# A hybrid decoder step: another order of the mixers, and convolution taps as ScalarE products with wide VectorE adds

## The chip, the cores and the metric

The kernel runs on one core of a Trainium2 chip. The metric is the time of one execution on the device in microseconds (us), lower being better; the time before is the median of three runs. A profile is one execution taken by the hardware profiler. The engines are TensorE (PE, with its weight loads PEld), VectorE (DVE), ScalarE (ACT), GpSimd (POOL) and SyncE (SP), which here only issues transfers. Each engine works through its own instructions in order and waits on semaphores for the others.

## What is computed

256 prompt rows and 8 sample rows, 264 in all, go through one layer of width D = 2048, everything in fp32:

```python
xn = rms_norm(x, g_mix)
z = xn @ w_in      # pool u 512 | lru x 1024 | gelu gate 1024 | conformer a 512 | conformer b 512
# A: trailing means over 2/4/8/16 rows minus the row, a 128x128 map per group, a scale, @ w_pool_br
# B: causal depthwise convolution, 4 taps -> gates -> recurrence h = a*h + b, times gelu, @ w_lru_br
gate_r, gate_i = sigmoid(xb @ w_a + b_a), sigmoid(xb @ w_x + b_x)
log_a = -8 * gate_r * softplus(-lam)
b = x * gate_i * sqrt(-expm1(2 * log_a))
# C: v = a * sigmoid(b) -> causal depthwise convolution, 31 taps -> LayerNorm -> swish -> @ w_conf_br
gates = sigmoid(xn @ w_gate + b_gate)
x = x + (g_a * y_pool + g_b * y_lru + g_c * y_conf) @ w_out
x = x + square(relu(rms_norm(x, g_mlp) @ w_up)) @ w_down
y = rms_norm(x, g_final)
```

The new rows of the states (pooling inputs, both convolutions' inputs, the recurrence's last h) are outputs too.

## The kernel before

Everything on the chip is transposed: channels on the 128 partitions, the 264 rows along the free axis, so a product is a 128x128 weight tile with a 128x264 moving tile, summed in one of eight PSUM banks.

**The weight stream.** All dense weights come as chunks of 128x1024 (two k tiles for four output tiles). `weight_plan` lists the groups of chunks in the order in which TensorE goes through them: 56 chunks of `w_in`, then gates, branch projections, `w_out`, `w_up`, `w_down`. fp32 precision comes from splitting: ScalarE casts a chunk to its high part `whi` (`split`, L148), VectorE subtracts that to get the low part `wlo` (L149), and `mm3` (L152 to L154) makes three products per tile: high x high, high x low, low x high. A chunk is 24 products. The split of chunk i+3 is issued at chunk i (`AHEAD`); the rings of high and low parts have four slots (`NHI`), that of raw weights six, and SP loads pairs of chunks by `dma_pair`.

**x at the start.** `x_tile` splits one k tile of x into `A` (L228 or L230, and L231) and forms its squares, on GpSimd for the first four tiles and on ScalarE after (L262), summed on GpSimd (L264, L266). After chunk 9 `rms_close` multiplies the total by a matrix of ones on TensorE, and ScalarE and VectorE make the inverse root `rstd` of it (a seed by Ln and Exp and a Newton step, L215 to L218). The first group of `w_in`, the conformer's b, is finished before `rstd` exists: its evacuation is a copy (L432), and GpSimd scales it afterwards (L436).

**Background work.** What the mixers do between products is put in four queues of stages (`stage`): each task has an engine and a planned cost. At every chunk `run_bg` adds an income to each engine's credit (1.3 us for ScalarE, 1.4 for VectorE, 2.4 for GpSimd) and issues tasks in order while the credit lasts; a stage begins at least one chunk after the one before it, unless its gap is 0. `later(n, fn)` issues something n chunks on. The finished evacuations and gates take their cost off by `spend`. None of this is decided at run time: it fixes the order in which each engine gets its instructions.

- `lru_conv`: three of four taps are scalar_tensor_tensor operations on VectorE, one per channel tile (L317).
- `conf`: of 30 taps (beside the first), 14 (`TAPS`) are such operations on VectorE (L455) and 16 are products on ScalarE (L460) with sums on GpSimd (L463).
- `lru_tail`: a and sqrt(1 - a*a) are made of tanh and a reciprocal on VectorE (L395), products of two tiles on GpSimd (L377), the scan on VectorE (L380). `gelu` multiplies on GpSimd (L413).
- `pooling`: four doubling adds on GpSimd (L559), differences on VectorE (L571 to L576); `grp_mm` is the group map.

The order of `w_in` before: conformer b, conformer a, lru x (two groups), pool, gelu (two groups). The gate matrices' blocks of the recurrence (`lru_gate_mm`) follow chunks of the gelu groups (`LRU_AT`). Gates and projections then alternate; `branch_evac` multiplies a projection by its gate, GpSimd adds the branches up (L621), and the sum is split for `w_out`.

**The end.** The last products are three with the matrix of ones (L833), which sum the squares of the result. ScalarE and VectorE make the inverse root, VectorE scales the result in seven pieces (L842), and SP sends each one out (L843).

Of the kernel before, what the change touches and what calls it, by code (L numbers as in the profile page):

```python
# [308 lines left out]

# [622 lines left out]
```

## Time and profile before

| | |
|---|---|
| median of 3 runs | 1448.97 us (1448.65 to 1449.99) |
| the profiled execution's span | 1448.0 us |
| TensorE busy | 1407.7 us, 11418 products |
| VectorE busy | 850.1 us, 1060 instructions |
| ScalarE busy | 684.4 us, 931 instructions |
| GpSimd busy | 230.8 us, 235 instructions |

How to read the profile's lines: "L149 DVE TENSOR_TENSOR wlo<-raw,whi 128x1024 ... x480" is a group of instructions of line 149 on VectorE that write the tile wlo from raw and whi; then come their busy time, the mean ns of one, and the idle time of that engine before them with what ended it. A row of three durations with slashes gives the shortest, median and longest ns. A line of digits shows the span in 40 equal slices, each digit the busy share in tenths; PEclk is the granted TensorE clock in tenths. A row of a stretch gives its start and end, its length, and the busy time and instruction count of each engine. A timeline row begins with the start and the time taken, in us. A row of a wait names the engine, tile and line that waited, what ended the wait, and the total, the count and the longest in us. Products are pipelined and their ends modelled, so a busy TensorE isn't always TensorE at its full rate.

### The profile page before, as it was taken

What the parts mean: (1) busy time and instruction counts of PE and PEld (TensorE: products, weight loads), DVE (VectorE), ACT (ScalarE), POOL (GpSimd) and SP (SyncE); (2) the same over time, 40 slices, a digit from 0 to 9 for tenths busy, and PEclk for the clock granted to TensorE, in tenths of its full rate; (3) what the DMA queues carried; (4) which work ended last, traced back from release to release, by engine and by line L of the source; (5) the groups of instructions that cost most, each with busy time, mean ns of one, the idle gap of its engine ahead of it and who ended that gap; (6) DMA issues with size and microseconds to landing.
All of it is one profiled execution on the core that took longest, in us unless ns stands there. A gap on an engine that the chain in (4) does not pass through costs nothing.

```text
span 1448.0 us, 26716 instructions
## 1 busy us (share of the span) xinstructions
PE 1407.7 (97%) x11418; PEld 1400.4 (97%) x11418; DVE 850.1 (59%) x1060; ACT 684.4 (47%) x931; POOL 230.8 (16%) x235
## 2 busy tenths in 40 slices
PE   8988889999999999999999999999999999999996
PEld 7987889999999999999999999999999999999996
DVE  8599978855654545565655445454455554454543
ACT  6665468455444434354544334453334533354543
POOL 5577641432220200211000000000000000000011
PEclk9999999999999999999999999999999999999998
DMA  7533445555565555555555555555555555555551
GB/s 274 196 126 136 141 145 188 204 175 175 179 218 186 175 175 180 188 186 176 175 178 182 189 180 175 178 181 187 184 175 175 179 188 187 175 176 178 185 189 62
DMA packets 38567, 256.96 MB, mean 177 GB/s; under 512 B 4272, under 2 KB 5040, under 8 KB 9008
## 3 DMA queue, kind: packets, MB, share of 16 engines
q1 hardware_dynamic: 38304, 254.21, 52.0%
q8 instruction: 89, 1.46, 0.4%
q0 software_dynamic: 144, 1.04, 0.2%
q14 instruction: 30, 0.25, 0.0%
HBM read 252.03 MB, written 3.21 MB: 176 GB/s over the span
## 4 chain that ended last, share of the span: by engine, by line
PE 89%; DVE 7%; issue 2%; ACT 1%; DMA 0%; SPq 0%; DVEq 0%; ACTq 0%
PE acc L154 30%; PE acc L152 30%; PE acc L153 30%; DVE wlo L149 3%; DVE G L455 2%; DVE G L317 1%; DMA GX<-x_dram 0%; ACT whi L148 0%; DVE GX L842 0%; DVE A L231 0%; DVE L L342 0%; ACT G L312 0%; ACT A L230 0%; ACT G L450 0%; SPq L135 0%
## 5 line engine op out<-in xcount | busy, mean ns | idle before, releaser
L149 DVE TENSOR_TENSOR wlo<-raw,whi 128x1024 fp32r<-128x1024 f32 (+1 forms) x480 | 600.5, 1252 | 569.5 <-ACT whi L148 566.4
L148 ACT CAST whi<-raw 128x1024 fp32r<-128x1024 f32 (+1 forms) x480 | 497.7, 1038 | 688.4 <-PE acc L153 667.3
L154 PE MATMUL acc<-A,wlo 128*128 128x264 f32 x2236 | 640.9, 287 | 16.3 <-DVE wlo L149 16.2
L152 PE MATMUL acc<-A,whi 128*128 128x264 f32 x2236 | 640.8, 287 | 6.5 <-DVE tmp L406 5.9
L153 PE MATMUL acc<-A,whi 128*128 128x264 f32 x2236 | 638.6, 286 | 3.4 <-DVE A L231 3.4
L154 PEld LDWEIGHTS acc<-A,wlo 128*128 128x128 f32 x2236 | 424.7, 190 | 19.8 <-DVE wlo L149 19.8
L152 PEld LDWEIGHTS acc<-A,whi 128*128 128x128 f32 x2236 | 424.5, 190 | 7.0 <-issue 6.8
L153 PEld LDWEIGHTS acc<-A,whi 128*128 128x128 f32 x2236 | 425.4, 190 | 5.2 <-DVE A L231 5.1
L152 PE MATMUL acc<-mrg,whi 128*128 128x264 f32 x768 | 218.8, 285 | 0.0
L154 PE MATMUL acc<-mrg,wlo 128*128 128x264 f32 x768 | 218.5, 284 | 0.0
L153 PE MATMUL acc<-mrg,whi 128*128 128x264 f32 x768 | 218.1, 284 | 0.0
L154 PE MATMUL acc<-L,wlo 128*128 128x264 f32 x656 | 187.0, 285 | 0.9 <-DVE wlo L149 0.9
L152 PE MATMUL acc<-L,whi 128*128 128x264 f32 x656 | 186.5, 284 | 0.0
L153 PE MATMUL acc<-Q,whi 128*128 128x264 f32 x644 | 182.7, 284 | 0.0
L667 POOL TENSOR_TENSOR G<-G 128x264 f32<-128x264 f32 x28 | 25.7, 917 | 811.8 <-ACT G L665 810.9
L153 PEld LDWEIGHTS acc<-mrg,whi 128*128 128x128 f32 x768 | 145.1, 189 | 0.0
L154 PEld LDWEIGHTS acc<-mrg,wlo 128*128 128x128 f32 x768 | 144.9, 189 | 0.0
L152 PEld LDWEIGHTS acc<-mrg,whi 128*128 128x128 f32 x768 | 144.7, 188 | 0.0
L154 PEld LDWEIGHTS acc<-L,wlo 128*128 128x128 f32 x656 | 123.5, 188 | 1.1 <-DVE wlo L149 1.1
L152 PEld LDWEIGHTS acc<-L,whi 128*128 128x128 f32 x656 | 123.4, 188 | 0.0
L153 PEld LDWEIGHTS acc<-Q,whi 128*128 128x128 f32 x644 | 121.5, 189 | 0.0
L621 POOL TENSOR_TENSOR G<-G 128x264 f32<-128x264 f32 x32 | 31.0, 999 | 228.4 <-DVE G L618 228.4
(154 smaller groups left out, 870.1 us busy)
## 6 DMA issues: line engine op xcount, KB each, us to landing
raw<-wall_dram SPq DMA_DIRECT2D x230, 1024.0 KB, 4.9
raw<-wall_dram SPq DMA_DIRECT2D x11, 512.0 KB, 7.6
GX<-x_dram SPq DMA_DIRECT2D x7, 264.0 KB, 7.8
raw<-wall_dram SPq DMA_DIRECT2D x7, 256.0 KB, 3.2
y_dram<-GX SPq DMA_DIRECT2D x2, 528.0 KB, 2.8
so_dram<-st POOLq DMA_DIRECT2D x1, 1018.0 KB, 6.9
st<-st_dram SPq DMA_DIRECT2D x1, 912.0 KB, 8.0
y_dram<-GX SPq DMA_DIRECT2D x3, 132.0 KB, 1.8
```

The lines of the kernel that those rows point to most:

```text
L148: nc.scalar.copy(h[:, s], r[:, s])
L149: nc.vector.tensor_tensor(lo[:, s], r[:, s], f(h[:, s]), op=ALU.subtract)
L152: nc.tensor.matmul(ps[:, :N], whi_t, xh, start=first, stop=False)
L153: nc.tensor.matmul(ps[:, :N], whi_t, xl, start=False, stop=False)
L154: nc.tensor.matmul(ps[:, :N], wlo_t, xh, start=False, stop=last)
L317: nc.vector.scalar_tensor_tensor(XC[:, ct, :TP], el[:, ct, k:k + TP], par[:, w:w + 1], XC[:, ct, :TP], op0=ALU.mult, op1=ALU.add)
L455: nc.vector.scalar_tensor_tensor(VC[:, ct, :TP], vext[:, ct, k:k + TP], par[:, w:w + 1], VC[:, ct, :TP], op0=ALU.mult, op1=ALU.add)
L621: nc.gpsimd.tensor_tensor(t, t, G[:, (1 - g % 2) * 12 + br * 4 - 4 + m, :], op=ALU.add)
L667: nc.gpsimd.tensor_tensor(sq2, sq2, t, op=ALU.add)
```

## The change

- The order of `w_in` becomes lru x (two groups), pool, gelu (two groups), conformer b, conformer a. The gates are regrouped: the conformer's come last, and the four conformer projections stand together before `w_out`. The recurrence's gate blocks all lie in the second gelu group.
- The taps of both convolutions become products on ScalarE, one per channel tile, into two alternating tiles; VectorE adds each set of four channel tiles with one wide instruction (`gather`).
- In the recurrence the reciprocals go: with u = tanh(-log(a) / 2) as before and a itself from an exponential on ScalarE, sqrt(1 - a*a) is (1 + a) sqrt(u), and a for the scan is 1 - (1 + a) u; the multiplications move from GpSimd to VectorE, as do those of `gelu` and of the conformer's b.
- Squares of x are no longer formed in `x_tile` but at chunks 5 to 8, four tiles at a time on ScalarE (`x_squares`), with VectorE adds; `x_rms` folds them after chunk 9. The first group's evacuation is now a copy of lru x, scaled afterwards by `lru_x_scale`.
- Queues are three with a fixed priority, planned costs are raised, and ScalarE's income is 1.6 until the recurrence is done, then 1.3 (VectorE's 1.4, then 1.0).
- Partial sums of the branches get tiles of their own (`partial`), the merged sum and the MLP's hidden halves go to other tiles (`A`, `LH`).
- After the last products with the matrix of ones, 32 products into a bank that nobody reads (`probe`) are issued.

The diff, cut to its core:

```diff
-LRU_AT = ((3, 5), (3, 7), (4, 1), (4, 3))  # chunks of w_in that the blocks of the LRU gates follow
-TAPS = 14      # conformer taps on the vector engine
...
+LRU_AT = ((4, 1), (4, 3), (4, 5), (4, 6))
...
-    groups = [("w_in", 0, 16, m) for m in (6, 5, 1, 2, 0, 3, 4)]
-    groups += [("w_gate", 0, 16, br * 4 + g) for g in (0, 1) for br in range(3)]
+    groups = [("w_in", 0, 16, m) for m in (1, 2, 0, 3, 4, 6, 5)]
     for g in range(4):
-        if g >= 2:
-            groups += [("w_gate", 0, 16, br * 4 + g) for br in range(3)]
-        groups += [("w_pool_br", 0, 4, g), ("w_lru_br", 0, 8, g), ("w_conf_br", 0, 4, g)]
+        groups += [("w_gate", 0, 16, t) for t in ((0, 4, 1), (5,), (2, 6), (3, 7))[g]]
+        groups += [("w_pool_br", 0, 4, g), ("w_lru_br", 0, 8, g)]
+    groups += [("w_gate", 0, 16, 8 + g) for g in range(4)]
+    groups += [("w_conf_br", 0, 4, g) for g in range(4)]
...
-    queues = {"pool": [], "lru": [], "conf": [], "conf2": []}
+    queues = {"lru": [], "pool": [], "conf": []}
     ready_at = dict.fromkeys(queues, 0)
     credit = {"act": 0.0, "dve": 0.0, "pool": 0.0}
-    income = {"act": 1.3, "dve": 1.4, "pool": 2.4}
+    income = {"act": 1.6, "dve": 1.4, "pool": 2.4}
...
+        if "lru" in done:
+            income.update(act=1.3, dve=1.0)
...
+    sq4 = G[:, 20:24, :]
     def x_tile(k):
         split_scaled(A[:, k, :], A[:, 16 + k, :], X[:, k, :], GX[:, k:k + 1], k < 2)
-        t = sq_tot if k == 0 else G[:, 21 + k % 3, :]
-        if k >= 4:
-            nc.scalar.activation(t, X[:, k, :], AF.Square)
-        else:
-            nc.gpsimd.tensor_tensor(t, X[:, k, :], X[:, k, :], op=ALU.mult)
-        if k:
-            nc.gpsimd.tensor_tensor(sq_tot, sq_tot, t, op=ALU.add)
-    # ---- softplus(-lambda) * LRU_C / 2
+    def x_squares(j):
...
+        t = sq4 if j == 0 else G[:, 4 * (j % 2):4 * (j % 2) + 4, :]
+        nc.scalar.activation(t, X[:, 4 * j:4 * j + 4, :], AF.Square)
+        spend(act=1.1)
+        def add():
+            nc.vector.tensor_tensor(sq4, sq4, t, op=ALU.add)
+            spend(dve=1.25)
+        if j:
+            later(1, add)
+    def x_rms():
+        nc.vector.tensor_tensor(sq4[:, 0:2, :], sq4[:, 0:2, :], sq4[:, 2:4, :], op=ALU.add)
+        nc.vector.tensor_tensor(sq4[:, 0, :], sq4[:, 0, :], sq4[:, 1, :], op=ALU.add)
+        spend(dve=1.2)
+        rms_close(sq4[:, 0, :])
+        later(1, lru_x_scale)
...
+    def lru_x_copy(ct, ps):
+        nc.vector.tensor_copy(el[:, ct, 3:], ps[:, :TP])
+        nc.vector.tensor_copy(st_lc[:, ct, :, 3], ps[:, TP:N])
+        spend(dve=0.5)
+    def lru_x_scale():
+        for d, r in ((el[:, 0:4, 3:], rstd[:, None, :TP]), (st_lc[:, 0:4, :, 3], rstd[:, None, TP:])):
+            nc.vector.tensor_tensor(d, d, r.to_broadcast([P, 4, d.shape[2]]), op=ALU.mult)
+        spend(dve=1.4)
+        lru_conv(range(4))
...
+        def product(ct, k, dst):
             w = w0 + 4 * ct + k
-            nc.vector.scalar_tensor_tensor(XC[:, ct, :TP], el[:, ct, k:k + TP], par[:, w:w + 1], XC[:, ct, :TP],
-                                           op0=ALU.mult, op1=ALU.add)
-        stage("lru", "act", 0.4, [lambda ct=ct: first(ct) for ct in cts])
-        stage("lru", "dve", 0.41, [lambda ct=ct, k=k: tap(ct, k) for k in range(3) for ct in cts], 0)
+            nc.scalar.activation(dst[:, ct, :TP], el[:, ct, k:k + TP], AF.Copy, scale=par[:, w:w + 1])
+        def gather(src):
+            nc.vector.tensor_tensor(XC[:, cs, :TP], XC[:, cs, :TP], src[:, cs, :TP], op=ALU.add)
+        stage("lru", "act", 0.5, [lambda ct=ct: first(ct) for ct in cts], 0)
+        for k in range(3):
+            dst = (RA, GEL)[k % 2]
+            stage("lru", "act", 0.5, [lambda ct=ct, k=k, d=dst: product(ct, k, d) for ct in cts], 0 if k == 0 else 1)
+            if k:
+                stage("lru", "dve", 1.25, [lambda d=(RA, GEL)[1 - k % 2]: gather(d)], 0)
+        stage("lru", "dve", 1.25, [lambda: gather(RA)])
...
+        if ct % 2:
+            def times():
+                nc.vector.tensor_tensor(XC[:, ct - 1:ct + 1, :], XC[:, ct - 1:ct + 1, :], TM[:, ct - 1:ct + 1, :],
+                                        op=ALU.mult)
+                spend(dve=0.71)
+            later(1, times)
...
+        def decay(ct):
+            nc.scalar.activation(RA[:, ct, :], RA[:, ct, :], AF.Exp, scale=sp[:, 8 + ct:9 + ct])
+        def reset():
+            nc.gpsimd.memset(TM[:, :, 0:1], 1.0)
+            nc.gpsimd.memset(RA[:, :, 0:1], 0.0)
         def root(c):
-            nc.scalar.activation(TM[:, two(c), :], TM[:, two(c), :], AF.Sqrt, scale=4.0)
+            if not S:
+                scratch()
+            nc.scalar.activation(S[0][:, two(c), :], TM[:, two(c), :], AF.Sqrt)
...
+        def wide(c, dst, x):
+            nc.vector.scalar_tensor_tensor(dst[:, two(c), :], RA[:, two(c), :], 1.0, x[:, two(c), :],
+                                           op0=ALU.add, op1=ALU.mult)
         def a_of(c):
-            nc.vector.tensor_scalar(RA[:, two(c), :], RA[:, two(c), :], 2.0, -1.0, op0=ALU.mult, op1=ALU.add)
-        def times(c, t):
-            nc.gpsimd.tensor_tensor(TM[:, two(c), :], TM[:, two(c), :], t[:, two(c), :], op=ALU.mult)
+            nc.vector.tensor_scalar(TM[:, two(c), :], TM[:, two(c), :], -1.0, 1.0, op0=ALU.mult, op1=ALU.add)
+        def times(c):
+            nc.vector.tensor_tensor(RA[:, two(c), :], RA[:, two(c), :], XC[:, two(c), :], op=ALU.mult)
...
-        stage("lru", "act", 0.4, [lambda ct=ct: tanh(ct) for ct in range(8)])
-        stage("lru", "pool", 0.1, [lambda: nc.gpsimd.memset(TM[:, :, 0:1], 1.0)])
-        stage("lru", "act", 0.55, [lambda c=c: nc.scalar.activation(RA[:, two(c), :], TM[:, two(c), :], AF.Copy, bias=1.0)
-                                   for c in range(4)], 0)
-        stage("lru", "act", 0.55, [lambda c=c: root(c) for c in range(4)], 0)
-        stage("lru", "dve", 0.9, [lambda s=s: nc.vector.reciprocal(s, s) for ct in range(8)
-                                  for s in (RA[:, ct, :N // 2], RA[:, ct, N // 2:])])
-        stage("lru", "pool", 1.26, [lambda c=c: times(c, RA) for c in range(4)])
-        stage("lru", "pool", 1.26, [lambda c=c: times(c, XC) for c in range(4)], 0)
+        c4 = range(4)
+        stage("lru", "act", 0.52, [lambda ct=ct: tanh(ct) for ct in range(8)], 0)
+        stage("lru", "act", 0.52, [lambda ct=ct: decay(ct) for ct in range(8)])
+        stage("lru", "pool", 0.2, [reset])
+        stage("lru", "act", 0.65, [lambda c=c: root(c) for c in c4])
+        stage("lru", "dve", 0.75, [lambda c=c: wide(c, TM, TM) for c in c4], 0)
+        stage("lru", "dve", 0.43, [lambda c=c: a_of(c) for c in c4], 0)
+        stage("lru", "dve", 0.75, [lambda c=c: wide(c, RA, S[0]) for c in c4], 0)
+        stage("lru", "dve", 0.71, [lambda c=c: times(c) for c in c4], 0)
         mark("lru", "b_term")
-        stage("lru", "dve", 0.35, [lambda c=c: a_of(c) for c in range(4)])
-        stage("lru", "dve", 0.6, [lambda ct=ct: scan(ct) for ct in range(8)])
-        stage("lru", "pool", 1.0, [sample])
+        stage("lru", "dve", 0.69, [lambda ct=ct: scan(ct) for ct in range(8)])
+        stage("lru", "pool", 1.5, [sample])
...
+        nc.vector.tensor_tensor(SG[:, ct, :], ps[:, :N], rstd, op=ALU.mult)
+        spend(dve=0.43)
+        if ct == 3:
+            later(1, lambda: nc.scalar.activation(SG, SG, AF.Sigmoid))
+            later(2, scaled)
+    def scaled():
+        nc.vector.tensor_tensor(SG, SG, rstd[:, None, :].to_broadcast([P, 4, N]), op=ALU.mult)
+        spend(dve=1.25)
...
-        def gather(dst, src, ct):
-            nc.gpsimd.tensor_tensor(dst[:, ct, :TP], dst[:, ct, :TP], src[:, ct, :TP], op=ALU.add)
-        tmp = qtmp[:, 7 * W:7 * W + 992].rearrange("p (c b k) -> p c b k", c=4, b=8)
+        def gather(src):
+            nc.vector.tensor_tensor(VC[:, :, :TP], VC[:, :, :TP], src[:, :, :TP], op=ALU.add)
...
-        stage(q, "dve", 0.41, [lambda ct=ct, k=k: tap(ct, k) for k in range(TAPS) for ct in g4])
-        for k in range(TAPS, 30):
-            dst = SG if k == TAPS else GEL[:, k % 2 * 4:k % 2 * 4 + 4, :]
-            stage("conf2", "act", 0.4, [lambda ct=ct, k=k, d=dst: product(ct, k, d) for ct in g4])
-            if k > TAPS:
-                stage("conf2", "pool", 0.7, [lambda ct=ct, d=dst: gather(SG, d, ct) for ct in g4], 0)
-        mark("conf2", "conf2")
-        need(q, "conf2")
-        mark(q, "conv")
-        stage(q, "pool", 0.7, [lambda ct=ct: gather(VC, SG, ct) for ct in g4], 0)
+        stage(q, "act", 0.5, [lambda ct=ct: start(ct) for ct in g4])
+        stage(q, "dve", 1.4, [sums])
+        for k in range(30):
+            stage(q, "act", 0.5, [lambda ct=ct, k=k: product(ct, k, (CT, SG)[k % 2]) for ct in g4], 0 if k else 1)
+            if k:
+                stage(q, "dve", 1.25, [lambda k=k: gather((CT, SG)[1 - k % 2])])
+        stage(q, "dve", 1.25, [lambda: gather(SG)])
...
+        if br == 1:
+            nc.gpsimd.tensor_tensor(partial(k), t, gate_tile(0, g, m), op=ALU.add)
+            spend(pool=0.8)
         if br == 2:
-            if not M:
-                M.extend(cpool.tile([P, 8, N], F32R, name=f"mrg{i}", tag=f"B{i}") for i in range(4))
-            hi, lo = bpart(k)
-            later_split(hi, lo, t, 1)
+            nc.gpsimd.tensor_tensor(t, t, partial(k), op=ALU.add)
+            spend(pool=0.8)
+            later_split(A[:, k, :], A[:, 16 + k, :], t, 1)
...
+        if 5 <= i < 9:
+            x_squares(i - 5)
         if i == 9:
-            rms_close(sq_tot)
+            later(0, x_rms)
...
+    probe = acc()
+    for n in (N, 128, 400, 512):
+        for j in range(8):
+            nc.tensor.matmul(probe[:, :n], whi[:, j % 4, j * P:(j + 1) * P],
+                             A.rearrange("p a n -> p (a n)")[:, :n], start=True, stop=True)
```

More of the change, by code (lines that the diff above doesn't have):

```diff
@@ L96, in hybrid_step @@
     B = [cpool.tile([P, 8, N], F32, name=f"tmp{i}", tag=f"B{i}") for i in range(4)]
-    L = cpool.tile([P, 16, N], F32R, name="L")
+    L = cpool.tile([P, 16, N], F32R, name="L", tag="L")
     G = cpool.tile([P, 24, N], F32, name="G")
@@ L103, in hybrid_step @@
     eps = cpool.tile([P, 1], F32, name="eps")
-    sp = cpool.tile([P, 8], F32, name="sp")
+    sp = cpool.tile([P, 16], F32, name="sp")
     gfin = cpool.tile([P, KD], F32, name="gfin")
@@ L296, in hybrid_step, with LH @@
     W = 15 + TP
-    H, GEL, RA, TM = B
+    TM, GEL, RA, _ = B
+    H = RA
+    l_at = []
+    def LH(s):
+        if not l_at:
+            l_at.append(cpool.tile([P, 16, N], F32R, name="LH", tag="L"))
+        return l_at[0][:, s, :]
     def two(c):
         return slice(2 * c, 2 * c + 2)
+    def lru_x_copy(ct, ps):
[7 more added lines that the diff above has]
+        lru_conv(range(4))
     def lru_x_evac(ct, ps):
@@ L339, in stage_split @@
     def stage_split(q, n, hi, lo, x, gap=1):
-        stage(q, "act", 0.55, [lambda i=i: nc.scalar.copy(hi(i), x(i)) for i in range(n)])
-        stage(q, "dve", 0.62, [lambda i=i: nc.vector.tensor_tensor(lo(i), x(i), f(hi(i)), op=ALU.subtract)
+        stage(q, "act", 0.65, [lambda i=i: nc.scalar.copy(hi(i), x(i)) for i in range(n)])
+        stage(q, "dve", 0.71, [lambda i=i: nc.vector.tensor_tensor(lo(i), x(i), f(hi(i)), op=ALU.subtract)
                                for i in range(n)], gap)
@@ L351, in lru_gate_mm @@
     def lru_gate_mm(ct, c, j):
-        assert "xc" in done and (ct < 3 or "conv" in done)
+        assert "xc" in done
         hi, lo = whi[:, c % NHI, :], wlo[:, c % NHI, :]
@@ L431, in cb_evac @@
     def cb_evac(ct, ps):
-        nc.vector.tensor_copy(SG[:, ct, :], ps[:, :N])
-    def cb_scale():
-        for ct in range(4):
-            nc.gpsimd.tensor_tensor(SG[:, ct, :], SG[:, ct, :], rstd, op=ALU.mult)
-        later(1, lambda: [nc.scalar.activation(SG[:, ct, :], SG[:, ct, :], AF.Sigmoid) for ct in range(4)])
-        later(2, lambda: [nc.gpsimd.tensor_tensor(SG[:, ct, :], SG[:, ct, :], rstd, op=ALU.mult) for ct in range(4)])
+        nc.vector.tensor_tensor(SG[:, ct, :], ps[:, :N], rstd, op=ALU.mult)
[6 more added lines that the diff above has]
+        spend(dve=1.25)
     def ca_evac(ct, ps):
@@ L451, in start @@
                                  scale=par[:, wc + 31 * ct + 30:wc + 31 * ct + 31])
-        def tap(ct, k):
-            w = wc + 31 * ct + k
-            nc.vector.scalar_tensor_tensor(VC[:, ct, :TP], vext[:, ct, k:k + TP], par[:, w:w + 1], VC[:, ct, :TP],
-                                           op0=ALU.mult, op1=ALU.add)
         def product(ct, k, dst):
@@ L584, in grp_mm @@
     def grp_mm(c):
-        assert {"pool", "conf rows"} <= done
+        assert "pool" in done
         hi, lo = whi[:, c % NHI, :], wlo[:, c % NHI, :]
@@ L598, in bpart, with gate_tile, partial @@
     def bpart(k):
+        if not M:
+            M.extend(cpool.tile([P, 8, N], F32R, name=f"xn2{i}", tag=f"B{i}") for i in range(4))
         return M[k // 8][:, k % 8, :], M[2 + k // 8][:, k % 8, :]
+    def gate_tile(br, g, m):
+        if br == 2:
+            return G[:, 4 * g + m, :]
+        if br and g % 2:
+            return GEL[:, m, :]
+        return G[:, g % 2 * 8 + br * 4 + m, :]
+    def partial(k):
+        return (TM if k < 8 else RA)[:, k % 8, :]
     def gate_evac(br, g, m, ps):
-        assert {0: "normed", 1: "swished", 2: "conf"}[br] in done
-        assert g == 0 or {"b_term", "grp"} <= done
-        t = G[:, (1 - g % 2) * 12 + br * 4 + m, :]
+        assert {"b_term", "grp"} <= done and (br != 1 or g % 2 == 0 or "lru" in done) and ("conf" in done or br < 2 or g < 3)
+        t = gate_tile(br, g, m)
         nc.vector.tensor_tensor(t, ps[:, :N], rstd, op=ALU.mult)
@@ L729, in after @@
         if name == "w_in":
-            if m in (1, 2):
-                lru_conv(range(4 * m - 4, 4 * m))
-                if m == 2:
-                    lru_conv_sample()
-                    stage_split("lru", 4, hi_two(L), lo_two(L), lambda c: XC[:, 2 * c:2 * c + 2, :])
-                    mark("lru", "xc")
+            if m == 2:
+                lru_conv(range(4, 8))
+                lru_conv_sample()
+                stage_split("lru", 4, hi_two(L), lo_two(L), lambda c: XC[:, 2 * c:2 * c + 2, :])
+                mark("lru", "xc")
             elif m == 5:
@@ L743, in after @@
                     gelu(2)
-                    need("lru", "pool")
-                    stage_split("lru", 4, hi_two(L), lo_two(L), lambda c: GEL[:, 2 * c:2 * c + 2, :])
+                    stage_split("lru", 4, lambda c: LH(two(c)), lambda c: LH(slice(8 + 2 * c, 10 + 2 * c)),
+                                lambda c: GEL[:, two(c), :])
                     mark("lru", "lru")
@@ L806, in hybrid_step @@
                     fn(m, pss[m])
-                if gi:
-                    after(gi)
-                else:
-                    later(4, cb_scale)
+                after(gi)
         elif kind == "lru":
```

74 lines of the change are left out of this document (36 added, 38 removed).

## The prediction

> **What bounds the kernel now.** I read the summary and the forty slices first, then the busy time by stretches, then what TensorE waited for.
>
> ```profile
> span 1448.0 us, 26716 instructions
> PE 1407.7 (97%) x11418; PEld 1400.4 (97%) x11418; DVE 850.1 (59%) x1060; ACT 684.4 (47%) x931; POOL 230.8 (16%) x235
> PE   8988889999999999999999999999999999999996
> DVE  8599978855654545565655445454455554454543
> POOL 5577641432220200211000000000000000000011
> PEclk9999999999999999999999999999999999999998
> ```
>
> TensorE is busy nearly everywhere, so only its gaps can be won: at the left edge, in slices 3 to 6 (where DVE shows 9 and POOL 5 to 7), and at the end. Busy time hides pipelined gaps, so I count products per stretch:
>
> ```profile
> 0.00:30.00 30.00, 24.22 (x160) 21.82 (x161) 24.58 (x29) 20.08 (x39) 19.04 (x26) 1.00 0.80 280
> 30.00:66.00 36.00, 36.00 (x297) 35.94 (x296) 21.46 (x34) 18.04 (x25) 16.63 (x35) 1.00 0.60 209
> 66.00:218.00 152.00, 129.18 (x970) 125.30 (x969) 137.71 (x189) 88.10 (x153) 94.75 (x86) 0.94 0.42 140
> 218.00:254.00 36.00, 36.00 (x299) 36.00 (x298) 29.08 (x38) 28.89 (x42) 5.36 (x5) 1.00 0.51 180
> 254.00:1400.00 1146.00, 1146.00 (x9414) 1145.93 (x9413) 616.90 (x746) 511.04 (x648) 89.21 (x78) 1.00 0.54 182
> 1434.58 1.91 PE L833 MATMUL acc<-G,ones 128*128 128x264 f32 x6
> ```
>
> The columns are PE, PEld, DVE, ACT and POOL with counts, the granted clock, the DMA share, GB/s. In the 1146 us stretch 9414 products give 0.1217 us each: a chunk of 24 lasts 2.92 us. At that rate the 970 products between 66 and 218 us need 118.1 us of 152: **33.9 us are lost there**. In the first 30 us, 144 products (160 less 16 of warm-up) need 17.5 us: 12.5 lost. The end, from L833 to 1448.0, is 13.4 us. The other two stretches lose nothing. The plan's 11,388 products at 0.1217 us are 1386 us, and 1386 + 33.9 + 12.5 + 13.4 = 1446, so this accounts for the span.
>
> ```profile
> PE acc L154 <- DVE wlo L149: 17.1, 17, 2.6
> PE acc L152 <- DVE tmp L406: 5.9, 1, 5.9
> PE acc L153 <- DVE A L231: 3.4, 8, 0.9
> L149 DVE TENSOR_TENSOR wlo<-raw,whi 128x1024 fp32r<-128x1024 f32 x40 | 57.7, 1442 | 14.5 <-ACT whi L148 14.4
> L455 DVE SCALAR_TENSOR_TENSOR G<-tmp,par,G 128x256 f32<-128x256 f32 x56 | 38.7, 742 | 0.0
> L317 DVE SCALAR_TENSOR_TENSOR G<-tmp,par,G 128x256 f32<-128x256 f32 x24 | 21.1, 931 | 0.0
> L463 POOL TENSOR_TENSOR G<-G,tmp 128x256 f32<-128x256 f32 x60 | 63.3, 1088 | 22.3 <-ACT tmp L460 22.2
> ```
>
> Every one of these TensorE waits is for VectorE: low parts of weights (L149), one evacuation (L406), low parts of x (L231). VectorE has 137.7 us of work in a stretch whose products need 118, so it is the bound there. It also works slowly: the same operations in quiet places take
>
> ```profile
> L149 DVE TENSOR_TENSOR wlo<-raw,whi 128x1024 fp32r<-128x1024 f32 x68 | 83.8, 1232 | 94.3 <-ACT whi L148 94.3
> L455 DVE SCALAR_TENSOR_TENSOR G<-tmp,par,G x56: 467/710/2205, 73.5 to 182.4; 128x256 f32<-128x256 f32 x56
> ```
>
> 1232 ns between 400 and 600 us, against 1442 ns in the L149 row of 66 to 218 us, and a tap can take 467 ns, against means of 742 and 931. The difference is 40 x 0.21 + 56 x 0.275 + 24 x 0.464 = 35 us of VectorE time, and GpSimd is busy 94.75 us in that stretch: about 0.37 us lost per GpSimd microsecond.
>
> **The change, part by part.** Prices first:
>
> ```profile
> L342 DVE TENSOR_TENSOR Q<-G,Q 128x528 fp32r<-128x528 f32 x6 | 4.0, 701 | 0.0
> L380 DVE TENSOR_TENSOR_SCAN tmp<-tmp,tmp 128x256 f32<-128x256 f32 x8 | 5.2, 688 | 0.0
> L406 DVE TENSOR_TENSOR tmp<-acc,rstd 128x264 f32<-128x264 f32 x8 | 3.0, 424 | 0.1
> L395 DVE RECIPROCAL tmp<-tmp 128x132 f32<-128x132 f32 x16 | 14.8, 947 | 0.0
> L368 ACT ACTIVATE tmp<-tmp,sp 128x264 f32<-128x264 f32 x8 | 3.7, 522 | 0.0
> L208 ACT ACT_TABLE_LOAD x3 | 3.8, 1283 | 0.1
> L460 ACT ACTIVATE tmp<-tmp,par 128x256 f32<-128x256 f32 x60 | 26.0, 499 | 0.0
> L148 ACT CAST whi<-raw 128x1024 fp32r<-128x1024 f32 x469 | 491.1, 1048 | 679.9 <-PE acc L153 664.7 <-issue 12.5 <-DVE wlo L149 1.9
> L559 POOL TENSOR_TENSOR qtmp<-qtmp 128x1080 f32<-128x1080 f32 x1 | 6.0, 5963 | 8.7 <-DVE st L539 8.7
> L149 DVE TENSOR_TENSOR wlo<-raw,whi x480: 677/1225/2544, 5.6 to 1424.0; 128x1024 fp32r<-128x1024 f32 x158, 128x512 fp32r<-128x512 f32 x2
> ```
>
> *Conformer taps.* Removed from VectorE: 56 taps (38.7 us), and from GpSimd 60 adds (63.3 us). Added: 30 adds over all four channel tiles, 4 x 256 columns. No row shows a strided 1024-column add of this kind; the quiet L149 (two inputs, 1024 columns) is the nearest, so 1.23 us each, 37 us in all. The bounds are two 528-column operations (1.40) and L149's longest, 2.54. Products on ScalarE rise from 64 to 120: 56 x 0.499 = 28 us. What matters is the place: the conformer's group is now last of w_in, so its taps run beside the gate groups. There a tap wants 2.0 us of ScalarE from an income that becomes 1.3 per chunk, and one 1.23 us add: about one tap in two chunks, thirty taps in some 80 chunks (up to chunk 150 or so), and the conformer's projection comes only at chunk 182. Per chunk VectorE then does 1.23 (split) and at most one 1.23 add, or four evacuations (1.7) at a group's end: up to 2.9 of 2.92 us in single chunks, about 2.0 on average. So TensorE hides it. ScalarE there: 1.05 + 1.3 = 2.35 of 2.92.
>
> *The recurrence's stretch,* chunk 10 to about 66: 51 full chunks and five half ones, 156 us of products. VectorE's work by rows: splits 51 x 1.232 + 5 x 0.69 = 66; evacuations of six groups about 13; six conv adds 7.5; 16 two-tile products, splits and gate products at 0.70, 11; the eight wide (1 + r) steps, priced as L342, 6; scans 5.5; pooling differences, a, sums and scalings about 10. Together 119. GpSimd keeps the pooling adds (10 us), softplus and small steps, about 23 us for 95 before; at 0.37 that costs VectorE 8.5. So 128 of 156, or 82%, where it was 137.7 for 118. The reciprocals, 16 of 0.95 us, are gone; an exponential per channel tile on ScalarE takes their place (8 x 0.52). VectorE stops being the bound and the 33.9 us go, the half-clock windows inside them too.
>
> *What is late next.* A split may lag: its ScalarE half starts when a slot comes free at the start of chunk i and is needed at chunk i+3, so 8.76 - 1.05 - 1.23 = 6.5 us of lag are covered. My walk through the plan's credits leaves VectorE at most 4 us late (chunks 9 and 65) and ScalarE 3 to 4 (chunks 42 to 46, 65 to 70, a table load of 1.28 us in it). The gate blocks at chunks 40 and 42 stand closer together, and their four banks wait for ScalarE's sigmoids. I allow three waits of 1.0 us, the mean of the 17 above: **+3.0**, with 0 and 15 (below) as bounds. The four conformer projections in a row need 2 x 1.23 + 8 x 0.42 = 5.8 us of VectorE in 5.84: covered, if GpSimd's adds beside them add no more than 1.6 each.
>
> *x statistics later.* The sixteen squares and their GpSimd adds leave the start. VectorE is busy 24.6 of the first 30 us, on slow operations:
>
> ```profile
> L231 DVE SCALAR_TENSOR_TENSOR A<-GX,A x16: 480/948/990, 5.2 to 31.4; 128x264 fp32r<-128x264 f32 x16
> 5.33 1.20 PE L752 MATMUL acc<-A,whi 128*128 128x264 f32 x8 [0.50 <-DVE A L228]
> 9.21 0.62 ACT L148 CAST whi<-raw 128x512 fp32r<-128x512 f32 x1 [3.13 <-DMA raw<-wall_dram]
> 20.83 1.78 DVE L149 TENSOR_TENSOR wlo<-raw,whi 128x1024 fp32r<-128x1024 f32 x1
> ```
>
> A chunk there costs 1.78 + 2 x 0.95 = 3.7 us of VectorE, above 2.92; without GpSimd 1.23 + 2 x 0.48 = 2.2. Of the 12.5 us lost, 5.3 pass before the first product, and some 2.5 while the second chunk's weights arrive (the cast at 9.21); of the rest I take **-3.5** (bounds 0 and -5). The price comes at chunk 9: the ones product now waits for VectorE. From the chunk's start: high part 1.05, low part 1.23, add of the last squares 1.23, folds 0.70 and 0.42, so 4.6, against 2.92 of products: **+1.8** (0 to 4). The Newton step then holds VectorE while ScalarE loads a table, but chunk 13's low part still lands 3 us early.
>
> *GpSimd, SP, DMAs.* No transfer is added; the weights come in another order at the same rate. The states' way out stays at chunk 140, behind the same GpSimd steps.
>
> *The spare products.* Output transfers are still being issued at 1439.36 + 4.90 = 1444:
>
> ```profile
> 1439.36 4.90 SPq L843 DMA_DIRECT2D y_dram<-GX  x7
> ```
>
> 8 each of 264, 128, 400 and 512 columns are 10,432 columns: at 0.1217 us per 264, 4.8 us. They stand behind the last ones products, which end at 1434.58 + 1.91 = 1436.5, and end at 1441.3, under the tail of ScalarE, VectorE and output transfers to 1448: **0**. If that cover fails, +4.8.
>
> [...] Clock rows first:
>
> ```profile
> 78.00:82.00 4.00, 2.24 (x10) 2.24 (x11) 4.00 (x5) 2.44 (x5) 4.00 (x5) 0.72 0.00 0
> 186.00:190.00 4.00, 2.21 (x10) 2.24 (x11) 4.00 (x8) 0.00 (x0) 3.21 (x3) 0.50 0.41 106
> ```
>
> After crowded waits the clock is halved for a while. [...] The trace shows halving around 80 us, though no wait on L149 passed 2.6 us, so I keep a halved window as a rival.
>
> The pooling's 5.96 us GpSimd add ran beside low parts, of which none took over 2.54 us. [...]
>
> **Sum and rivals.** 1448.0 - 33.9 + 3.0 + 1.8 - 3.5 + 0 = 1415.4 us of span; the three timed runs' median, 1448.97, stands 1.0 above the profiled span, so **1416.4 us** (chance 0.60, own range 1410 to 1423).
>
> - *VectorE or in-order ScalarE chains still starve the splits in the recurrence's stretch* (0.25). For: total VectorE work hardly falls (the wide adds replace the taps), conv products wait for adds and block the next cast behind them. Against: 82% use, and lag within cover. A GpSimd slowdown of all remaining work as bad as before, and a wait in each of 15 places at 1.0 us, give +12: 1428; bounds 1423 to 1432.
> - *A halved clock after chunk 9* (0.04): 3.4 us at half rate, +1.7, 1418.
> - *The end waits for the spare products* (0.04): +4.8, 1421; were each column to cost what L833's two-pass products cost (1.91 / 792), 25 us, past the tail by 14, 1430.
> - *The start does not gain* because arrivals bound it (0.04): 1420.
> - *Slower* (0.03): each conformer add waits for four products that wait for the add before, and holds back a cast and a low part behind it. It decides from 32.6 / 30 = 1.1 us of stall per tap; at 2.6 us, the longest wait above, 30 taps cost 78 and the time is 1416 + 78 = 1494. Against: successive tiles alternate, and the plan puts a chunk between.
>
> **How the numbers follow.** The range takes the forecast, the small rivals and most of the first: 1409 to 1430 (lower end: no stall left, the start's full 5 us). A measurement here can tell about 0.2%, 3 us, from no change; only the slower case, or one between, gets near: faster 0.96, same 0.01, slower 0.03.
>
> **What would show it.** Right: products per 36 us at 300 between 72 and 217, GpSimd near 2 there, no half clock, a single wait of the ones product near 40 us, spare products ended before the output. Wrong: waits on L149 in the gate groups (about 240 to 520 us), or on ScalarE's sigmoids near 120 us; a late end of the statistics; Ln behind the last spare product.

## The result, and the profile after

| | before | after |
|---|---|---|
| median of the runs | 1448.90 us | 1423.67 us (1423.39 to 1424.49) |
| span of the profiled execution | 1448.0 us | 1421.7 us |

The ratio of the times is 0.9823, 95% interval 0.9809 to 0.9837: 25 us less, inside the range, 7.3 us above the sum of 1416.4. The first part of the page after, and the busy time by the same stretches as before:

```profile
span 1421.7 us, 26648 instructions
PE 1403.1 (99%) x11450; PEld 1399.8 (98%) x11450; DVE 834.0 (59%) x1036; ACT 718.8 (51%) x1004; POOL 98.8 (7%) x118
PE   9799999999999999999999999999999999999998
DVE  6676688766766657656555444555454545455543
POOL 0240010101101102111000000000000000000011
PEclk9899999999999999999999999999999999999999
```

```profile
0.00:30.00 30.00, 27.29 (x195) 26.03 (x196) 19.77 (x33) 20.58 (x31) 0.54 (x7) 1.00 0.88 323
30.00:66.00 36.00, 27.33 (x209) 26.94 (x208) 20.29 (x32) 18.27 (x31) 5.15 (x12) 0.86 0.46 157
66.00:218.00 152.00, 152.00 (x1251) 152.00 (x1250) 114.40 (x164) 96.42 (x145) 25.53 (x30) 1.00 0.53 179
```

VectorE's total hardly moved (850.1 to 834.0 us) and ScalarE's rose; GpSimd fell from 230.8 to 98.8. At 0.1217 us a product the middle stretch holds 1251 products, all that fit into 152 us: **the 33.9 us lost there are gone to the last one.** The first 30 us lose 8.2 in place of 12.5 (179 products without the warm-up). But a hole has opened between 30 and 66 us: 209 products are 25.4 of 36 us, **10.6 lost** where nothing was lost before. Three rows of TensorE's list of waits, and the chain of work that ended last, around that hole:

```profile
PE acc L222 <- DVE G L276: 8.7, 1, 8.7
PE acc L546 <- POOL G L540: 0.8, 1, 0.8
PE acc L153 <- DVE wlo L148: 0.2, 1, 0.2
```

```profile
29.94 7.88 DMA st<-st_dram
37.82 0.02 issue
37.85 0.17 DVE st L326
...
39.23 1.16 DVE G L268
...
45.77 0.44 DVE G L276
46.22 0.14 issue
46.35 1.22 PE acc L222 x2
```

The waits on low parts, 17.1 us before, are 0.2. By far the longest wait left is one of 8.7 us, of the ones product (L222) on the fold of the squares (L276); the other 1.9 us of the hole are products at a halved clock behind it (0.50 from 46.4 to 50 us). The chain says where the wait comes from. `lru_x_copy` evacuates the first group while `rstd` is missing. Its second instruction (L326) writes the sample rows into the state tile, and that tile is still being loaded: SP issued the load at 29.94 us and it took 7.88. VectorE's next instructions, the adds of the squares, the low parts and the folds, stand behind that copy and the rest of the evacuation: they ran from 39.1 to 46.2 us. A small wait near 450 us (L546, the conformer's ones product on GpSimd's total) costs about 1.3 us: the 12 us there hold 90 products, where a full stretch of 12 us holds 101. The sum closes: 1448.0 - 33.9 - 4.3 + 10.6 + 1.3 = 1421.7.

### The profile page after: what moved, and what is told of

The parts are those of the page before. It is cut to its first block, busy times and chain, and to the rows that moved or that the text cites. A ratio compares the mean times of both kernels' runs of the same rounds, so it can differ in the third digit from the quotient of the medians.

```text
span 1421.7 us, 26648 instructions
## 1 busy us (share of the span) xinstructions
PE 1403.1 (99%) x11450; PEld 1399.8 (98%) x11450; DVE 834.0 (59%) x1036; ACT 718.8 (51%) x1004; POOL 98.8 (7%) x118
## 4 chain that ended last, share of the span: by engine, by line
PE 95%; DMA 2%; DVE 1%; POOL 0%; ACT 0%; SPq 0%; issue 0%; DVEq 0%; ACTq 0%
PE acc L153 32%; PE acc L151 32%; PE acc L152 32%; DMA raw<-wall_dram 1%; DMA GX<-x_dram 1%; DMA st<-st_dram 1%; DVE GX L916 0%; POOL tmp L688 0%; DVE wlo L148 0%; DVE G L268 0%; SPq L134 0%; ACT whi L147 0%; SPq L138 0%; PE acc L222 0%; POOL G L540 0%
## 5 line engine op out<-in xcount | busy, mean ns | idle before, releaser
L151 PE MATMUL acc<-A,whi 128*128 128x264 f32 x1980 | 565.5, 286 | 1.2 <-DVE A L228 0.6
L152 PE MATMUL acc<-A,whi 128*128 128x264 f32 x1980 | 563.1, 284 | 0.2
L151 PEld LDWEIGHTS acc<-A,whi 128*128 128x128 f32 x1980 | 374.0, 189 | 1.7 <-issue 0.8
L152 PEld LDWEIGHTS acc<-A,whi 128*128 128x128 f32 x1980 | 374.8, 189 | 0.8 <-DVE A L231 0.6
L151 PE MATMUL acc<-xn,whi 128*128 128x264 f32 x1024 | 291.9, 285 | 0.0
L153 PE MATMUL acc<-xn,wlo 128*128 128x264 f32 x1024 | 291.3, 285 | 0.0
L152 PE MATMUL acc<-xn,whi 128*128 128x264 f32 x1024 | 290.8, 284 | 0.0
L152 PEld LDWEIGHTS acc<-xn,whi 128*128 128x128 f32 x1024 | 193.5, 189 | 0.0
L153 PEld LDWEIGHTS acc<-xn,wlo 128*128 128x128 f32 x1024 | 193.1, 189 | 0.0
L151 PEld LDWEIGHTS acc<-xn,whi 128*128 128x128 f32 x1024 | 193.0, 189 | 0.0
L153 PE MATMUL acc<-LH,wlo 128*128 128x264 f32 x640 | 182.3, 285 | 0.0
L151 PE MATMUL acc<-LH,whi 128*128 128x264 f32 x640 | 182.0, 284 | 0.0
L153 PEld LDWEIGHTS acc<-LH,wlo 128*128 128x128 f32 x640 | 120.4, 188 | 0.0
L151 PEld LDWEIGHTS acc<-LH,whi 128*128 128x128 f32 x640 | 120.4, 188 | 0.0
```

The lines of the kernel that those rows point to most:

```text
L151: nc.tensor.matmul(ps[:, :N], whi_t, xh, start=first, stop=False)
L152: nc.tensor.matmul(ps[:, :N], whi_t, xl, start=False, stop=False)
L153: nc.tensor.matmul(ps[:, :N], wlo_t, xh, start=False, stop=last)
```

## The experiments

Each kernel was timed against the kernel before on the same chip, so ratios are what compares across them; the changed kernel's is 0.9823.

**The spare products.** Edit: the `probe` loop removed.

> The changed kernel without its 32 spare products at the end. Theory (they lie under the tail: they ended at 1415.4 us of a span of 1421.7 and the Ln step began at 1410.3, before them): 1423.7, within 1 us. Rival (the end waits for them, or their transfers of operands slow the last steps): 1418 to 1419, 4.8 to 5.5 less.

Measured 1423.73 us, ratio 0.9818 (0.9802 to 0.9835): no difference. The timeline of the changed kernel's end:

```profile
1408.34 1.91 PE L902 MATMUL acc<-G,ones 128*128 128x264 f32 x6
1409.90 5.51 PE L906 MATMUL acc<-A,whi 128*128 128x264 f32 x32
1410.29 0.48 ACT L209 ACTIVATE rstd<-acc,eps 128x264 f32<-128x264 f32 x1 [0.26 <-PE acc L902]
1413.13 4.91 SPq L917 DMA_DIRECT2D y_dram<-GX  x7
```

ScalarE's Ln starts 0.26 us after its ones product, as before the change, while the 32 spare products run beside it; they end at 1415.4, while the output transfers are still being issued (until 1418.0).

**The hole at 40 us.** Two kernels take away the copy's dependence in different ways, and one puts the squares back.

```diff
st_early:
-        if i == 6:
+        if i == 2:
             nc.sync.dma_start(st[:, :S_IN], st_in)
held_rows:
-        nc.vector.tensor_copy(st_lc[:, ct, :, 3], ps[:, TP:N])
+        nc.vector.tensor_copy(G[:, 16, 8 * ct:8 * ct + 8], ps[:, TP:N])
...
+        held = G[:, 16, 0:32].rearrange("p (c b) -> p c b", c=4)
+        for d, x, r in ((el[:, 0:4, 3:], el[:, 0:4, 3:], rstd[:, None, :TP]),
+                        (st_lc[:, 0:4, :, 3], held, rstd[:, None, TP:])):
...
sq_start: the squares of x_tile as before the change, rms_close on their total, x_squares and the folds removed
```

> The changed kernel with the load of the states issued at chunk 2 in place of chunk 6. Theory (the ones product waits 8.7 us because VectorE's copy of the sample rows waits 6.1 us for that load, and the clock is halved for some us after): the wait falls to about 1.8 us and the time to 1414 to 1416, if the 0.9 MB do not delay the weights; were they delayed by their own length, some 2 to 3 us at 325 GB/s, 1417. Rival (the wait is the squares' own chain of adds and folds, and the copy's wait only lies beside it): the wait stays above 6 us and the time above 1421.

> The changed kernel in which the first group's sample rows are copied to a spare tile and scaled from there into the states, so that the copy at chunk 7 does not need the states' load; no transfer moves. Theory: the ones product waits 1.5 to 2.5 us in place of 8.7, no half-clock stretch after it, time 1414 to 1415. Rival (squares' chain): wait above 6 us, 1421 or more. Between the two, a wait of 4 us and a half clock, 1418.

> The changed kernel with the squares of x back at the start, on GpSimd and ScalarE as before the change; all else as changed. Theory (later statistics won 4.3 us in the first 30 us and lost 10.6 between 30 and 66): the ones product does not wait, the start loses 12 to 12.5 us again, time 1417 to 1418, so that this part of the change cost 6 us net. Rival (the start's gain is from elsewhere): the start stays at 8 us lost and the time is 1413.

Measured: st_early 1416.77 us (0.9773, 0.9759 to 0.9788), held_rows 1416.66 (0.9774, 0.9760 to 0.9789), sq_start 1417.68 (0.9781, 0.9766 to 0.9795). The wait of the ones product, in this order, from the three kernels' lists of waits:

```profile
PE acc L222 <- DVE G L276: 3.1, 1, 3.1
```

```profile
PE acc L222 <- DVE G L276: 2.2, 1, 2.2
```

```profile
PE acc L222 <- DVE st L331: 1.0, 1, 1.0
```

Both remedies take 7 us, without touching the squares, so the load is the cause and the squares' own chain isn't: with held_rows its wait is 2.2 us, near the 1.8 that was worked out for the chain alone. The times came out 1 to 2 us above what I expected. In st_early the squares' chain still starts 1.4 us later than in held_rows (33.6 for 32.2 us), and the wait is 3.1. In held_rows part is the clock, halved for a while after a wait of only 2.2 us; these are its rows of 36 to 42 and 42 to 48 us, with clocks of 0.90 and 0.82:

```profile
36.00:42.00 6.00, 3.76 (x25) 3.52 (x24) 4.05 (x6) 2.70 (x4) 0.00 (x0) 0.90 0.42 165
42.00:48.00 6.00, 6.00 (x43) 6.00 (x42) 3.13 (x5) 2.85 (x5) 0.00 (x0) 0.82 0.51 175
```

At half rate (the 0.50 that rows of the changed kernel show behind its wait), 0.10 and 0.18 of 6 us stand for twice that, 3.4 us in all. In held_rows 263 products lie between 30 and 66 us, so 4.0 us are lost there: 2.2 of waiting and 1.8 by the clock.

sq_start has 150 products in the first 30 us, so loses 11.7 us there again, and 286 between 30 and 66, losing 1.2. The later statistics thus won 3.5 us at the start and, as built, cost 9.4 behind it: 6 us net. I had expected no wait of the ones product there; the 1.0 us is put down to the copy of the sample rows, which is L331 in that kernel and still waits 6.5 us for the states' load, only with no squares behind it.

**What bound the stretch from 66 to 218 us: VectorE's own work, or GpSimd beside it?** Both kernels are the kernel before with one edit:

```diff
b_wide:
-                stage("conf2", "pool", 0.7, [lambda ct=ct, d=dst: gather(SG, d, ct) for ct in g4], 0)
+                stage("conf2", "pool", 2.4, [lambda d=dst: nc.vector.tensor_tensor(
+                    SG[:, :, :TP], SG[:, :, :TP], d[:, :, :TP], op=ALU.add)], 0)
b_nosum:
-            if k > TAPS:
-                stage("conf2", "pool", 0.7, [lambda ct=ct, d=dst: gather(SG, d, ct) for ct in g4], 0)
```

> The kernel before, with the 15 sums of conformer products done as one wide VectorE add each in place of four GpSimd adds. Contention theory: GpSimd loses 60 x 1.09 = 65 us in the stretch from 66 to 218, which gives VectorE back some 23 us, and 15 x 1.23 = 18 us of adds come on top: VectorE work falls by 5, time 1442 to 1446. Rival (GpSimd costs VectorE nothing, only VectorE's own count matters): 18 us more, 1462 to 1468.

> The kernel before, without the 60 GpSimd adds that sum 15 of the 16 conformer products (15 of the 31 taps are left out of the convolution; their products are still made). VectorE's own instructions are the same. Contention theory: VectorE's work between 66 and 218 us falls by 60 x 1.09 x 0.37 = 24 us, from 138 to 114, below the 118 of the products: most of the 33.9 us goes, time 1420 to 1430. Rival (only VectorE's own count matters): 1447 to 1450.

Measured: b_wide 1436.32 us (0.9911, 0.9896 to 0.9926), b_nosum 1421.76 (0.9809, 0.9794 to 0.9824). Taking 60 GpSimd adds away, and no VectorE instruction, wins 27 us: as much as the whole change (25). The stretch of 66 to 218 us in b_wide and in b_nosum, and the low parts and taps of b_nosum in it by line:

```profile
66.00:218.00 152.00, 138.06 (x1085) 134.42 (x1084) 135.62 (x217) 102.28 (x174) 37.93 (x30) 0.99 0.47 155
66.00:218.00 152.00, 147.71 (x1198) 147.40 (x1198) 129.73 (x217) 112.73 (x188) 33.77 (x30) 0.99 0.52 172
```

```profile
L149 DVE TENSOR_TENSOR wlo<-raw,whi 128x1024 fp32r<-128x1024 f32 x48 | 61.2, 1276 | 22.6 <-ACT whi L148 22.5
L455 DVE SCALAR_TENSOR_TENSOR G<-tmp,par,G 128x256 f32<-128x256 f32 x56 | 26.1, 521 | 0.0
L317 DVE SCALAR_TENSOR_TENSOR G<-tmp,par,G 128x256 f32<-128x256 f32 x24 | 10.2, 479 | 0.0
```

The same 56 and 24 taps take 36.3 us where they took 59.8 (742 and 931 ns), and low parts 1276 ns for 1442. VectorE's busy time in the stretch fell less, to 129.7, because 217 instructions, not 189, now fit into it. In the kernel before, neither VectorE nor ScalarE waits for GpSimd in that stretch by the list of waits, so the adds held VectorE up by making its instructions longer, not by a dependency. b_wide shows the same trade with the sums kept: VectorE gets 15 more adds, and still the kernel gains 12.6 us, more than I had expected (3 to 7). It also shows the limit of the old order with all taps computed: 1085 products for 970 are 14.0 of the 33.9 us, and waits on low parts remain (11.1 us). Its adds confirm the price taken for the wide form:

```profile
L510 DVE TENSOR_TENSOR G<-G,tmp 128x1024 f32<-128x1024 f32 x15 | 18.2, 1216 | 0.0
```

**Form or place of the conformer's taps.** Both are the changed kernel with one edit:

```diff
dve_taps:
+        def tap(ct, k):
+            w = wc + 31 * ct + k
+            nc.vector.scalar_tensor_tensor(VC[:, ct, :TP], vext[:, ct, k:k + TP], par[:, w:w + 1], VC[:, ct, :TP],
+                                           op0=ALU.mult, op1=ALU.add)
         for k in range(30):
-            stage(q, "act", 0.5, [lambda ct=ct, k=k: product(ct, k, (CT, SG)[k % 2]) for ct in g4], 0 if k else 1)
-            if k:
-                stage(q, "dve", 1.25, [lambda k=k: gather((CT, SG)[1 - k % 2])])
-        stage(q, "dve", 1.25, [lambda: gather(SG)])
+            stage(q, "dve", 0.5, [lambda ct=ct, k=k: tap(ct, k) for ct in g4], 0 if k < 29 else 1)
pool_gather:
-            nc.vector.tensor_tensor(VC[:, :, :TP], VC[:, :, :TP], src[:, :, :TP], op=ALU.add)
+            nc.gpsimd.tensor_tensor(VC[:, :, :TP], VC[:, :, :TP], src[:, :, :TP], op=ALU.add)
```

(in pool_gather the 30 stages are planned at 2.4 us of GpSimd).

> The changed kernel, with the conformer's 30 taps in the old form (120 scalar_tensor_tensor on VectorE, one per channel tile) at the new place beside the gates; no product on ScalarE, no wide add. Theory (the place is what freed the stretch from 66 to 218 us; at the new place VectorE has room for either form): 120 x 0.47 = 56 us of VectorE for 37, no wait on low parts, 1423.7 within 1.5 us. Rival (the wide form is what counts): VectorE fills up in the gate groups, waits on low parts there, 5 to 20 us more.

> The changed kernel with the conformer's 30 wide adds on GpSimd in place of VectorE. Theory (GpSimd slows VectorE by about 0.37 us per us, but beside the gates VectorE has room): low parts there go from 1.23 to about 1.4 to 1.5 us on average, TensorE does not wait, 1423.7 within 2 us. Rival (GpSimd contention starves the low parts wherever it falls): waits on low parts, 10 us more or worse.

Measured: dve_taps 1422.44 us (0.9815, 0.9800 to 0.9829), pool_gather 1424.33 (0.9827, 0.9811 to 0.9844): neither differs from the changed kernel. At the new place VectorE takes 120 taps of the old form without a wait: 1860 products between 218 and 444 us, as in the changed kernel. With the adds on GpSimd it even takes heavier contention than I had expected (low parts of 1.4 to 1.5 us and no wait of TensorE): the low parts of pool_gather between 260 and 430 us, by line and with their spread, and its waits,

```profile
L148 DVE TENSOR_TENSOR wlo<-raw,whi 128x1024 fp32r<-128x1024 f32 x60 | 102.0, 1721 | 50.8 <-ACT whi L147 50.5
```

```profile
L148 DVE TENSOR_TENSOR wlo<-raw,whi x60: 1205/1226/3426, 259.0 to 427.5; 128x1024 fp32r<-128x1024 f32 x60
PE acc L153 <- DVE wlo L148: 1.8, 2, 1.6
```

are 40% longer on average than 1232 ns, single ones by 2.2 us, and TensorE waits 1.8 us in all. Part of this is hidden in the time, because pool_gather has no wait near 450 us (1.3 us). So the wide form isn't what the change gains by. What it gains by is that the conformer's taps and GpSimd's adds beside them are gone from a stretch that VectorE filled: leaving the adds out is worth 27 us (b_nosum), putting them on VectorE in the old order 12.6 (b_wide). How the rest divides between the taps and the other moves was not measured.

**The recurrence's products back on GpSimd.** pool_rec: the changed kernel with six wide convolution adds and 20 two-tile products issued on `nc.gpsimd` and planned there (2.4 us, and 1.2 or 1.8).

> The changed kernel with the recurrence's six wide convolution adds and its 20 two-tile products (gates, recurrence, gelu) on GpSimd in place of VectorE. Contention at 0.37: 53 us more of GpSimd cost VectorE 20 us, its own instructions fall by 21, so its use stays near 82% and TensorE does not wait: 1423.7 within 2 us. Rival (with GpSimd busy the stretch is bound by VectorE again, or the longer chain makes the gate products wait): waits on low parts or on the gates' input, 1430 or more.

Measured 1430.42 us (0.9869, 0.9853 to 0.9886): 6.7 us more, the rival, but not by VectorE's use. The whole loss lies between 70 and 82 us. Timeline rows there, of GpSimd, ScalarE, VectorE and TensorE:

```profile
68.73 7.26 POOL L355 TENSOR_TENSOR G<-G,tmp 128x1024 f32<-128x1024 f32 x3
71.16 1.71 ACT L352 ACTIVATE tmp<-tmp,par 128x256 f32<-128x256 f32 x4 [9.80 <-POOL G L355]
73.84 3.24 DVE L148 TENSOR_TENSOR wlo<-raw,whi 128x1024 fp32r<-128x1024 f32 x1 [11.21 <-ACT whi L147]
77.13 0.59 PE L153 MATMUL acc<-A,wlo 128*128 128x264 f32 x1 [2.77 <-DVE wlo L148]
```

The first wide add stands on GpSimd behind the softplus series, which ends at 68.7. ScalarE's next products reuse the tile that this add reads, so ScalarE stands for 9.8 us, and the casts of weights behind it with it; VectorE then has nothing to do for 11.2 us. TensorE lives for some chunks on what was split ahead and then runs dry: it waits 2.8 and 2.4 us, and the clock is 0.84 and 0.74 in the rows of 74 to 78 and 78 to 82 us. The rest of the stretch from 66 to 218 us loses nothing, though GpSimd is busy for 51.1 us of it in all.

**A better version.** held_early is held_rows with the squares at chunks 4 to 7 and the folds issued at chunk 8; best is that without the spare products and with the conformer's totals one chunk further ahead:

```diff
held_early (beside held_rows; x_fold holds the two folds that stood in x_rms):
...
-        if 5 <= i < 9:
-            x_squares(i - 5)
+        if 4 <= i < 8:
+            x_squares(i - 4)
+        if i == 8:
+            later(0, x_fold)
best (beside held_early, and without probe):
-        stage(q, "pool", 2.0, [lambda: total(VC)], 2)
+        stage(q, "pool", 2.0, [lambda: total(VC)], 3)
-        stage(q, "pool", 2.0, [lambda: total(SG)], 2)
+        stage(q, "pool", 2.0, [lambda: total(SG)], 3)
```

> held_rows with the squares at chunks 4 to 7 and the folds issued at chunk 8, one chunk ahead of the ones product. Theory: the remaining wait of 2.2 us and what is left of the halved clock go, 1416.7 - 2.2 - 1.0 = 1413 to 1414. Rival (the start is then bound elsewhere, ScalarE with squares among casts and x tiles): the wait moves to a low or high part, 1416 to 1417.

> held_early, without the spare products, and with the conformer's two totals one chunk further ahead of their ones products. Theory: the 0.8 us wait on GpSimd near 450 us goes as well, 0.5 to 1.3 us below held_early: 1412 to 1413.5. Rival: the same as held_early.

Measured: held_early 1413.96 us (0.9757, 0.9743 to 0.9772), best 1412.62 (0.9749, 0.9736 to 0.9762): 37 us below the kernel before as timed beside it, and 11 below the changed one. The two can't be told apart by time; in the trace the wait of L546 is gone and the stretch from 30 to 66 us of best holds 283 products for 209 (its ones product at chunk 9 still waits 1.4 us, 0.4 in held_early):

```profile
30.00:66.00 36.00, 34.57 (x283) 34.33 (x282) 27.09 (x46) 24.05 (x39) 12.54 (x26) 1.00 0.56 193
66.00:218.00 152.00, 152.00 (x1251) 152.00 (x1250) 115.08 (x161) 98.56 (x150) 19.23 (x17) 1.00 0.55 185
```

## Why the prediction held, and where it was off

- **VectorE is the bound between 66 and 218 us, because GpSimd slows it: held.** All 33.9 us came back, and b_nosum gets 27 us by taking only GpSimd's adds away. The rate of 0.37 us per GpSimd microsecond was too low for these adds: in b_nosum the 80 taps are 23.5 us shorter and 40 low parts, at 0.166 each, 6.6 us, for 61.0 us less of GpSimd, which makes about 0.5. So b_wide gained 12.6 us where the rate gave 3 to 7.
- **The place hides the taps: held.** dve_taps and pool_gather leave the time as it is.
- **Waits that remain, +3.0:** almost none is left (0.2 us on low parts); 1.3 us appeared near 450 us at a place that I hadn't named.
- **The start, -3.5:** -4.3 in the trace; sq_start, which undoes it, loses 3.5.
- **The price at chunk 9, +1.8 with 4 as its upper bound: this term failed.** It measured 10.6 us with the halved clock. The chain of adds and folds itself was about right (a wait of 2.2 us in held_rows; the parts listed for it, 4.6 less 2.92, make 1.7 and not 1.8). What was left out is the step before it on VectorE: the evacuation of the group that was moved to the front writes into the state tile, and the states' load was in the profile (8.0 us to landing, issued from SP behind weight loads that wait for slots). Before the change the first evacuation into that tile (L442) came at 62.7 us, long after it. The prediction said that no transfer is added, which was true, and didn't ask which instruction now needs one earlier.
- **Spare products, 0: held,** as no_spare shows.
- **A halved clock after chunk 9,** a rival at 0.04, came true behind the longer wait, in these stretches of the changed kernel (0.83, 0.50 and 0.82). Its 3.4 us at half rate are what the kernel before shows around 80 us: granted clocks of 0.89, 0.50, 0.50, 0.50 and 0.90 in the five rows of 1 us from 79 to 84 us. Its price of 1.7 us was right: 1.9 here (10.6 less the wait of 8.7), 1.8 in held_rows. The chance was too low: in held_rows a wait of 2.2 us, close to the one forecast, was enough.

```profile
36.00:42.00 6.00, 1.68 (x14) 1.47 (x13) 4.15 (x10) 1.51 (x2) 0.00 (x0) 0.83 0.02 7
42.00:48.00 6.00, 1.65 (x5) 1.47 (x6) 4.14 (x5) 2.17 (x3) 0.00 (x0) 0.50 0.51 175
48.00:54.00 6.00, 6.00 (x44) 6.00 (x43) 3.99 (x7) 2.82 (x6) 0.00 (x0) 0.82 0.23 70
```

- **ScalarE chains in order,** the mechanism of the largest rival, did not show in the recurrence's stretch of the changed kernel. The time alone would not have told: 1423.7 us lies just outside the forecast's own range (1410 to 1423) and inside that rival's (1423 to 1432). The trace decides against it, with all 1251 products in the stretch. pool_rec shows that the mechanism exists and what it takes: one wait of 9.8 us ahead of a cast.
- The measured time lies 2.0 us above the profiled span, where the sum added 1.0; that is the rest of the 7.3 us, beside the hole's 8.8 (10.6 - 1.8) and what the start (0.8) and the waits (1.7) gave back. In the runs that give both figures the time stands about 1.8 us above the span of the same execution, so the profile before was probably of an execution 0.8 us slower than the median, and that went into the sum. That some errors were of opposite sign helped the number, and was luck.

Whether a still smaller GpSimd load in the old order would have sufficed without moving the conformer, with all taps computed, wasn't tried beyond b_wide. The recurrence's new form wasn't taken back by itself either.

## What to carry to other kernels

Where VectorE is full, count GpSimd's busy time beside it before counting VectorE's instructions: moving work from GpSimd to VectorE can make both shorter (between 66 and 218 us of b_wide GpSimd is busy 37.9 us for 94.8 and VectorE 135.6 for 137.7, with 217 instructions for 189). When a step moves forward, list for each tile that it writes who still fills it, transfers first, and what stands behind the step on its engine; one copy of eight columns cost 7 us here. Where the bound engine had room, the form of the taps made no difference in time (dve_taps, 1422.4 us for 1423.7); a cast of weights behind a wait of 9.8 us did (pool_rec, 1430.4).

## What the runs showed of the hardware

- GpSimd's durations grow too. The pooling's 1080-column add took 5.96 us before and 1.99 in pool_rec:

```profile
L615 POOL TENSOR_TENSOR qtmp<-qtmp 128x1080 f32<-128x1080 f32 x1 | 2.0, 1987 | 2.8 <-DVE st L595 2.8
```

  In both cases shown here the instruction that started second was the one that took long. Before, the add started 0.09 us behind a low part, which took its usual 1.21 us, as these timeline rows show (two adds in the second).

```profile
155.24 1.21 DVE L149 TENSOR_TENSOR wlo<-raw,whi 128x1024 fp32r<-128x1024 f32 x1
155.33 7.63 POOL L559 TENSOR_TENSOR qtmp<-qtmp 128x1080 f32<-128x1080 f32 x2 [8.68 <-DVE st L539]
```

  Six VectorE instructions ran beside the 5.96 us of that add, the longest of 2.21 us. In pool_gather it was the other way round: one wide add took 2.40 us, close to the shortest of its kind (2.39), and the low part that started 1.61 us behind it took 1.87 us for 1.23 and ended 1.1 us after the add:

```profile
305.72 2.40 POOL L524 TENSOR_TENSOR G<-G 128x1024 f32<-128x1024 f32 x1 [3.68 <-ACT G L521]
307.33 1.87 DVE L148 TENSOR_TENSOR wlo<-raw,whi 128x1024 fp32r<-128x1024 f32 x1 [1.72 <-ACT whi L147]
```

  The longest low part there took 3.43 us.
- One wide GpSimd add of 1024 columns took 2.82 us on average in pool_gather, four of 256 columns 4 x 1.09 before; but VectorE was fuller beside the narrow ones (137.7 of 152 us, for 167.3 of 226 in pool_gather), and the shortest of each, 2.39 and 4 x 0.74, are closer.
- A single wait of 2.2 us (held_rows) was followed by a halved clock for 3.4 us, worked out above from its rows; one of 3.1 us (st_early) by none (clock 1.00 from 30 to 66 us). The kernel before has the same: the clock was 1.00 from 70 us up to this wait, and the row of 78 to 82 us with a clock of 0.72, which the prediction puts down to crowded waits, is what came behind it. The prediction's other row (186 to 190 us, clock 0.50) follows one wait of 5.9 us.

```profile
79.76 0.59 PE L154 MATMUL acc<-A,wlo 128*128 128x264 f32 x1 [2.17 <-DVE wlo L149]
```

- The first tile's VectorE scaling (L228) took 0.82 us before, with one of GpSimd's squares beside it, and 0.36 after, with none. Here VectorE started first (at 4.36 us, the square at 4.41), so the order of starting does not explain every case.
